# Conditioning vectors as row sums on VectorE, with an instruction order written out by hand

## The chip, the cores and the metric

The kernel runs on one core of a Trainium2 chip. The metric is the device time of one execution in microseconds (us), the median of several runs. A core has five engines that run side by side, each with its own queue in program order: TensorE (PE, matrix products; its weight loads are shown apart as PEld), VectorE (DVE), ScalarE (ACT), GpSimd (POOL) and SyncE (SP, which here sends the DMAs). All tensors are 32-bit floats. PE sums in PSUM, and everything else lives in SBUF with 128 partitions.

## The reference

One layer of a decoder trunk for one sequence of 512 tokens, width 1024. What matters here is the conditioning: a vector `c` of 1024 values gives six vectors of 1024.

```python
ada = (c @ w_ada[l] + b_ada[l])[:, None, :]          # w_ada: 1024 x 6144
sh1, sc1, gt1, sh2, sc2, gt2 = jnp.split(ada, 6, axis=-1)
h = rms_norm(x, norm1_w[l]) * (1.0 + sc1) + sh1
proj = h @ w_in[l]                                    # 1024 x 10016
...                                                   # two token mixers, gated
x = x + gt1 * ((g_att * y_att + g_rwkv * y_rwkv) @ w_o[l])
h = rms_norm(x, norm2_w[l]) * (1.0 + sc2) + sh2
x = x + gt2 * conv_ffn(h, w_up[l], conv_w[l], conv_b[l], w_down[l])
```

`sh1` and `sc1` are needed before the first product, `gt1` after the mixers, the rest still later. `w_ada` is 25 MB of a total of 127 MB that is read.

## The kernel before

**Products.** A 32-bit product is made of three: each operand is split into a high part (`hi`, rounded to a type that PE multiplies in one pass) and the remainder (`lo`), and `hi*hi`, `hi*lo` and `lo*hi` are summed in one PSUM bank. Splitting a weight tile costs a copy on ACT (`whi`) and a subtraction on DVE (`wlo`); the same is done to h (`hhi`, `hlo`). h is kept transposed, in eight chunks k of 128 features by 512 tokens.

**The start** (`start`, L608). x comes in four slices of 128 tokens, is normalised on ACT and DVE, and is turned on PE (`tr`). Meanwhile PE runs products on the identity whose result nobody reads (`warm`). `sh1` and `sc1` are made in four groups of two chunks: for a group eight DMAs of 256 KB bring w_ada rows (`araw`, L693, pieces of 1 KB), DVE multiplies each by its element of c and adds it to `acc` (L701, L703), and PE sums `acc` over the partitions with a column of ones (`ada<-few,acc`), which leaves a column per chunk; DVE adds the bias and makes `g1c` = (1 + sc1) * norm1_w (L727 to L729). ACT then makes a chunk of h from the turned x (L743) and `hhi` (L750), DVE makes `hlo` (L747), and the first products (`early`, L332 like all products) use each chunk as it comes, beside a part of the values (`v`).

**The other four vectors** (`ada_rest`, L512) are summed in the same way beside the attention part, from rows of 512 KB (L529, L531): for `sh2` and `sc2` again eight passes on PE, for the two gates four products with one output row each (`ada<-acc,few`), to which DVE adds the bias row before a DMA writes it to DRAM. The small vectors (biases, scales, convolution weights) come as rows from 17 DMAs and are turned into columns on PE (`vec`, L434 to L464).

**What sets the order.** Every step of the first two thirds is a task of a planner (`Plan`): engine, estimated duration, function, predecessors, priority, and buffers taken and given back. `Plan.run` plays the tasks through in time by the estimates and calls a task's function when its turn comes, which writes its instructions into the queues. `RANKS` moves the priority of named tasks, `HOLDS` holds back short PE steps (`few`) between long ones. On the chip each engine then runs its queue in that order, and semaphores keep the dependencies. The later parts (output projection, the gated MLP) are written in plain program order.

Of the kernel before, what the change touches and what calls it, by code (L numbers as in the profile page):

```python
# [39 lines left out]
class Task:  # L40
# [7 lines left out]
    ('ACT', '', '<lambda>', 200.0): -191.73,  # L48
    ('ACT', '', '<lambda>', 200.6): -134.73,
    ('ACT', '', 'l2_hi', 1.0): 88.76,  # L50
    ('ACT', '', 'r_hi', 200.1): 3.11,
    ('ACT', '', 'r_hi', 200.3): 21.71,
    ('ACT', 'exp', '<lambda>', 1.02): -19.52,
    ('ACT', 'exp', '<lambda>', 1.03): -33.04,
    ('ACT', 'gate hi', 'hi', 78.0): -74.13,
    ('ACT', 'k3 hi', 'hi', 49.0): 154.17,
    ('ACT', 'o', 'out', 1.03): 224.13,
    ('ACT', 'pr hi', 'hi', 88.0): -104.97,
    ('ACT', 'pts', 'turned', 1.0): 211.5,
    ('ACT', 'qk01', 'out', 1.0): 29.09,  # L60
    ('ACT', 'qk01 hi', 'hi', 12.0): 49.1,
    ('ACT', 'qk12 hi', 'hi', 17.0): -28.85,
    ('ACT', 'r4 hi', 'hi', 53.0): -52.65,
    ('ACT', 'v0 hi', 'hi', 42.0): 167.12,
    ('ACT', 'v12 hi', 'hi', 19.0): 218.37,
    ('ACT', 'v4 hi', 'hi', 54.0): 202.52,
    ('DMA', 'ada', 'load', 2.0): -35.02,
    ('DMA', 'ada', 'load', 3.0): -14.22,
    ('DMA', 'ada', 'load', 19.0): 1.45,
    ('DMA', 'ada', 'load', 25.0): -1.05,  # L70
    ('DMA', 'ada', 'load', 35.0): -1.19,
    ('DMA', 'gate', 'load', 64.0): 1.55,
    ('DMA', 'gate', 'load', 67.0): -2.21,
    ('DMA', 'gate', 'load', 68.0): 6.69,
    ('DMA', 'gate', 'load', 69.0): -6.31,
    ('DMA', 'gate', 'load', 73.0): 116.59,
    ('DMA', 'gate', 'load', 79.0): 160.33,
    ('DMA', 'lg', 'load', 38.0): -12.76,
    ('DMA', 'lg', 'load', 39.0): 1.1,
    ('DMA', 'pa', 'load', 81.0): 4.99,  # L80
    ('DMA', 'qk00', 'load', 4.0): -4.27,
    ('DMA', 'qk00', 'load', 5.0): -4.9,
    ('DMA', 'qk01', 'load', 11.0): -5.78,
    ('DMA', 'qk01', 'load', 25.0): -5.77,
    ('DMA', 'qk02', 'load', 29.0): 5.91,
    ('DMA', 'qk11', 'load', 27.0): 6.78,
    ('DMA', 'r7', 'load', 62.0): -1.38,
    ('DMA', 'rows', 'rows', 2.5): -19.57,
    ('DMA', 'rows', 'rows', 3.5): -7.21,
    ('DMA', 'v rows', 'v_load', 2.5): -6.43,  # L90
    ('DMA', 'v1', 'load', 45.0): -21.04,
    ('DMA', 'v2', 'load', 48.0): 13.86,
    ('DMA', 'v4', 'load', 54.0): -22.65,
    ('DMA', 'vec', 'load', 2.0): -50.64,
    ('DMA', 'x', 'load', 2.0): -53.8,
# [12 lines left out]
    ('DVE', 'ada', 'biased', 1.0): -46.21,
    ('DVE', 'ada', 'step', 1.5): 1.76,
    ('DVE', 'ada', 'step', 13.0): 32.5,  # L110
    ('DVE', 'ada', 'step', 15.0): 215.86,
    ('DVE', 'ada', 'step', 29.0): 61.6,
    ('DVE', 'pack', '<lambda>', 10.0): 154.57,
    ('DVE', 'qk01 lo', 'lo', 11.0): 43.99,
    ('DVE', 'qk01 lo', 'lo', 12.0): 19.2,
    ('DVE', 'qk02 lo', 'lo', 15.0): 160.78,
    ('DVE', 'qk10 lo', 'lo', 6.0): 20.02,
    ('DVE', 'r0 lo', 'lo', 41.0): -82.24,
    ('DVE', 'scan', '<lambda>', 200.1): -141.11,
    ('DVE', 'scan', '<lambda>', 200.4): -137.12,  # L120
    ('DVE', 'scan', '<lambda>', 200.7): -53.23,
    ('DVE', 'shift', '<lambda>', 1.0): 6.96,
    ('DVE', 'stat', '<lambda>', 1.02): -2.02,
    ('DVE', 'v lo', 'v_lo', 2.1): 43.03,
    ('DVE', 'v12 lo', 'lo', 19.0): -18.19,
    ('DVE', 'vec', '<lambda>', 1.0): 22.14,
    ('PE', '', '<lambda>', 0.0): -43.73,
    ('PE', 'early', '<lambda>', 10.6): 1.01,
    ('PE', 'gate', '<lambda>', 73.0): 6.63,
    ('PE', 'gate', '<lambda>', 75.0): -165.2,  # L130
    ('PE', 'gate', '<lambda>', 80.0): -14.65,
    ('PE', 'gate', '<lambda>', 81.0): 11.59,
    ('PE', 'gate', '<lambda>', 82.0): -91.61,
    ('PE', 'gate', '<lambda>', 83.0): 166.56,
    ('PE', 'gate', '<lambda>', 85.0): -83.89,
    ('PE', 'gate', '<lambda>', 87.0): 28.15,
    ('PE', 'k1', '<lambda>', 51.0): -49.98,
    ('PE', 'k3', '<lambda>', 57.0): 13.69,
    ('PE', 'pa', '<lambda>', 1.0): -0.19,
    ('PE', 'pa', '<lambda>', 90.0): -40.42,  # L140
    ('PE', 'pa', '<lambda>', 92.0): -19.64,
    ('PE', 'pa', '<lambda>', 95.0): 1.02,
    ('PE', 'pe', '<lambda>', 0.5): -74.3,
    ('PE', 'pe', 'first_pe', 0.5): -3.97,
    ('PE', 'pg', '<lambda>', 1.3): -85.89,
    ('PE', 'pg', '<lambda>', 1.4): -151.02,
    ('PE', 'pg', '<lambda>', 1.5): -8.13,
    ('PE', 'po', '<lambda>', 1.0): 2.71,
    ('PE', 'po', '<lambda>', 1.03): 3.37,
    ('PE', 'pt', '<lambda>', 1.4): 26.5,  # L150
    ('PE', 'pt', 'turn', 1.01): 0.03,
    ('PE', 'pt', 'turn', 1.02): 11.92,
    ('PE', 'pw', 'rates', 1.1): -1.11,
    ('PE', 'pw', 'rates', 1.2): 9.95,
# [2518 lines left out]
```

## Time and profile before

| | us |
|---|---|
| median of 3 runs | 1171.47 (1171.33 to 1172.0) |
| the profiled execution, its own time | 1172.75 |
| its span, first to last instruction | 1171.0 |
| w_ada in the chain that ended last | 2% of the span (DMA) |

A page of the profile gives each engine's busy time and number of instructions, then the chain of work that ended last, followed backwards. A group row reads: line, engine, operation, output and inputs, shapes, count | busy us, mean ns of one | idle time ahead of it and what ended it. A row of the timeline is: start, duration, engine, line, operation, names, count, and in brackets the idle time ahead. A row of stretches gives, for a window from A to B, the busy time of PE, PEld, DVE, ACT and POOL with their instructions, PE's granted clock, the share of the DMA engines and GB/s. A row of waits names who waited for whom: us in all, times, longest. Matmuls overlap, so their durations are longer than the distance between their starts.

### The profile page before, as it was taken

The numbers are of one execution on the slowest core, as the hardware profiler recorded it, in microseconds if no ns is written. First come the engines' busy times: TensorE is split into PE (matmuls) and PEld (weight loads), VectorE is DVE, ScalarE is ACT, GpSimd is POOL, SyncE is SP. The second block draws the span as 40 slices with busy tenths as digits, with TensorE's granted clock in tenths as the row PEclk, the third lists the DMA queues.
The fourth block names the chain that finished last, engine by engine and source line by source line (L and its number), as shares of the span: only waits on it lengthen the run. The fifth ranks groups of instructions, "written<-read, shape, count | busy, mean of one in ns | idle before, by whom it ended". The sixth has DMA issues, their size and how long they took to land.

```text
span 1171.0 us, 19239 instructions
## 1 busy us (share of the span) xinstructions
PE 1155.3 (99%) x7552; PEld 936.3 (80%) x7552; DVE 740.9 (63%) x1249; ACT 544.1 (46%) x1012; POOL 132.3 (11%) x271
## 2 busy tenths in 40 slices
PE   8999999999999999999999999999999999999997
PEld 8888888888788777777777777888888888888886
DVE  6788856324788978566997556744665666652236
ACT  5475433425476374464555653434444444432123
POOL 5010000000301013241002340023000000000001
PEclk9999999999999999999999999999999999999999
DMA  9765864111333332332243426621333333342231
GB/s 313 245 198 169 253 200 142 55 54 42 93 96 97 95 81 91 104 112 75 72 112 103 152 78 200 200 103 37 90 94 104 90 102 97 90 120 96 92 125 72
DMA packets 168330, 138.94 MB, mean 119 GB/s; under 512 B 8785, under 2 KB 150315, under 8 KB 168239
## 3 DMA queue, kind: packets, MB, share of 16 engines
q1 hardware_dynamic: 168095, 137.39, 38.7%
q8 instruction: 59, 0.97, 0.3%
q14 instruction: 32, 0.26, 0.1%
q10 hardware_dynamic: 144, 0.33, 0.1%
HBM read 127.39 MB, written 10.30 MB: 118 GB/s over the span
## 4 chain that ended last, share of the span: by engine, by line
PE 86%; DVE 7%; DMA 3%; issue 1%; ACT 1%; SPq 1%; POOL 0%; POOLq 0%; DVEq 0%; ACTq 0%
PE u L332 23%; PE o L332 13%; PE v L332 8%; PE qk L332 8%; PE pg L332 7%; PE pr L332 4%; PE k L332 4%; PE r L332 3%; PE pa L332 3%; DMA araw<-in_w_ada_dram 2%; PE pt L335 2%; PE xy L332 2%; PE sc L332 1%; PE xo L332 1%; PE po L332 1%
## 5 line engine op out<-in xcount | busy, mean ns | idle before, releaser
L378 DVE TENSOR_TENSOR wlo<-raw,whi 128x1024 fp32r<-128x1024 f32 x65 | 79.6, 1225 | 134.9 <-ACT whi L377 134.9
L332 PE MATMUL u<-h2hi,whi 128*128 128x512 f32 (+2 forms) x368 | 140.6, 382 | 0.0
L332 PE MATMUL u<-h2lo,whi 128*128 128x512 f32 (+2 forms) x368 | 140.6, 382 | 0.0
L332 PE MATMUL u<-h2hi,wlo 128*128 128x512 f32 (+2 forms) x368 | 140.5, 382 | 0.0
L1390 ACT CAST whi<-raw 128x1024 fp32r<-128x1024 f32 (+1 forms) x73 | 72.4, 993 | 103.4 <-PE qk L332 51.4
L377 ACT CAST whi<-raw 128x1024 fp32r<-128x1024 f32 x65 | 68.5, 1054 | 92.7 <-PE o L332 53.7
L1393 DVE TENSOR_TENSOR wlo<-raw,whi 128x1024 fp32r<-128x1024 f32 (+1 forms) x73 | 84.7, 1160 | 31.5 <-ACT whi L1390 30.6
L332 PEld LDWEIGHTS u<-h2lo,whi 128*128 128x128 f32 x368 | 69.1, 188 | 13.4 <-POOL h2lo L589 0.2
L332 PEld LDWEIGHTS u<-h2hi,wlo 128*128 128x128 f32 x368 | 69.1, 188 | 13.2
L332 PEld LDWEIGHTS u<-h2hi,whi 128*128 128x128 f32 x368 | 69.1, 188 | 12.9
L2488 DVE SCALAR_TENSOR_TENSOR u<-u,cols,u 128x511 f32<-128x511 f32 x88 | 65.7, 747 | 4.3 <-ACT u L2486 2.7
L332 PE MATMUL qk<-hhi,whi 128*128 128x512 f32 x160 | 63.3, 396 | 0.6 <-DVE qk L931 0.6
L332 PE MATMUL qk<-hhi,wlo 128*128 128x512 f32 x160 | 63.0, 394 | 0.0
L332 PE MATMUL qk<-hlo,whi 128*128 128x512 f32 x160 | 62.9, 393 | 0.0
L332 PE MATMUL o<-whi,fhi 128*128 128x512 f32 x144 | 56.1, 390 | 0.3 <-DVE u L2488 0.3
L332 PE MATMUL o<-wlo,fhi 128*128 128x512 f32 x144 | 56.0, 389 | 0.0
L332 PE MATMUL o<-whi,flo 128*128 128x512 f32 x144 | 56.0, 389 | 0.0
L332 PE MATMUL pg<-hlo,whi 128*128 128x512 f32 x128 | 52.0, 407 | 0.0
L332 PE MATMUL pg<-hhi,whi 128*128 128x512 f32 x128 | 51.6, 405 | 0.0
L332 PE MATMUL pg<-hhi,wlo 128*128 128x512 f32 x128 | 51.4, 403 | 0.0
L531 DVE SCALAR_TENSOR_TENSOR acc<-araw,cols,acc 128x1024 f32<-128x1024 f32 x28 | 35.9, 1282 | 17.6 <-DMA araw<-in_w_ada_dram 17.2
L2240 ACT CAST fhi<-u 128x512 fp32r<-128x512 f32 x22 | 13.7, 621 | 60.9 <-DVE u L2499 60.9
(462 smaller groups left out, 2776.3 us busy)
## 6 DMA issues: line engine op xcount, KB each, us to landing
raw<-in_w_in_dram SPq DMA_DIRECT2D x62, 512.0 KB
raw<-in_w_up_dram SPq DMA_DIRECT2D x44, 512.0 KB
araw<-in_w_ada_dram SPq DMA_DIRECT2D x32, 512.0 KB
raw<-in_w_down_dram SPq DMA_DIRECT2D x22, 512.0 KB
araw<-in_w_ada_dram SPq DMA_DIRECT2D x32, 256.0 KB
wvraw<-in_w_in_dram SPq DMA_DIRECT2D x20, 256.0 KB
raw<-in_w_rwkv_out_dram SPq DMA_DIRECT2D x8, 512.0 KB
raw<-in_w_o_dram SPq DMA_DIRECT2D x8, 512.0 KB
```

Source lines behind the costliest of these rows:

```text
L332: return self.nc.tensor.matmul(out, lhsT, rhs, start=start, stop=stop)
L335: self.nc.tensor.matmul(out, in_, self.ident[: in_.shape[0], : in_.shape[0]], is_transpose=True, start=start, stop=stop,)
L377: self.nc.scalar.copy(hl[0], raw)
L378: (lo_eng or self.nc.vector).tensor_tensor(hl[1], raw, hl[0], op=ALU.subtract)
L531: nc.vector.scalar_tensor_tensor(d["acc"], raw, ck, d["acc"], op0=ALU.mult, op1=ALU.add)
L1390: nc.scalar.copy(d["w"][0], d["raw"])
L1393: nc.vector.tensor_tensor(d["w"][1], d["raw"], d["w"][0], op=ALU.subtract)
L2240: self.nc.scalar.copy(hi, src)
L2488: nc.vector.scalar_tensor_tensor(u[:, d:], pu[:, : S - d], ch(c), u[:, d:], op0=ALU.mult, op1=ALU.add)
```

## The change

The two inputs are laid out before the launch (transposed and packed, no arithmetic): `w_ada` so that one output of the conditioning is one row of 1024 weights, 128 outputs to a slice of 512 KB; the small vectors as columns, in one array `vecs`, which two DMAs bring.

c is spread to all partitions (`cb`): a one-row load, two products with a row of ones, two copies on ACT. A slice of w_ada then gives 128 outputs in one DVE instruction, which multiplies by `cb` and adds along the row, starting from the bias (`ada_col`); a second, short instruction reads the accumulator out into the column. There is no `acc` and no `ada` product any more. `sh1` and `sc1` are made chunk by chunk, with two slices each. For k below 2 ACT writes `hhi` straight from PSUM, ahead of h itself; in the first group of weights the three products of a k are separate steps. `sh2` and `sc2` are put where `sh1` and `g1c` stood, and the gates go to DRAM as columns.

The planner still runs, but only to know which task runs on which engine: `AFTER` then moves single tasks behind others in an engine's list, and `MERGE`, a string with one letter a task, fixes in which order the engines' lists are written out. `RANKS` is another table. Smaller edits: one PSUM bank now holds `xy` and the state sum `w` and another `u`; `gt1b` is loaded earlier (in the gate stage, at m = 2); the first up products run in another order; the first eight down products too; 40 warming products and 12 more instead of 56.

```diff
 RANKS = {
-    ('ACT', '', '<lambda>', 200.0): -191.73,
...
 }
+AFTER = {
+    'ACT': (
+        "57:47 5:57 3:5 145:65 148:85 180:94 183:180 117:202 118:117 221:125 218:133 367:142 237:367 337:237 236:337 "
...
+MERGE = (
+    "dpddpppdapdpvagpdppadvgpappapdppppvpvpgdppvppappdpppavpvgpppdgappvpdppvpppdapppgapvpdapppdpvpappppppvadpppvpapp"
...
+    def issue(self, order):
+        for eng, moves in AFTER.items():
+            moves = [[int(x) for x in m.split(":")] for m in moves.split()]
+            moved = {u for u, _ in moves}
+            o = [t for t in order[eng] if t.uid not in moved]
+            for u, p in moves:
+                o.insert(o.index(self.tasks[p]) + 1 if p >= 0 else 0, self.tasks[u])
+            order[eng] = o
...
+        for c in MERGE:
+            t = next(next_[c])
+            assert not t.left, (t.uid, t.eng, t.name)
+            for u in t.users:
+                u.left -= 1
+            t.fn()
...
+    def ada_col(self, raw, col, m):
+        self.nc.vector.tensor_tensor_reduce(raw, raw, self.cb, 1.0, self.col["b_ada"][:, m : m + 1],
+                                            op0=ALU.mult, op1=ALU.add, accum_out=col)
...
     def ada_rest(self):
-                    nc.sync.dma_start(d["raw", k], self.w_ada[0][k * P : (k + 1) * P, part * D : (part + 1) * D])
+                    nc.sync.dma_start(d["raw", k], self.w_ada[part * KD + k])
...
-                        nc.vector.scalar_tensor_tensor(d["acc"], raw, ck, d["acc"], op0=ALU.mult, op1=ALU.add)
+                    self.ada_col(d["raw", k], d["col"][:, k : k + 1], part * KD + k)
...
-                        self.mm(d["ps"][:, j : j + 1], d["acc"][:, j * P : (j + 1) * P], self.ones[:, :1], j == 0, j == KD - 1)
...
-                        self.mm(d["ps", q][:1, :], self.ones[:, :1], d["acc"][:, q * 256 : q * 256 + 256], True, True)
...
+                prev = pl.add("DMA", 1.0, lambda d=d, name=name: nc.sync.dma_start(
+                    self.ada2[name][0].rearrange("(k p) -> p k", p=P), d["col"]), [prev], W_ + self.bodies, lag=2.0,
+                    marks=("att",), name="ada")
...
     def start(self):
+        def c_all(h):
+            d[h] = psp("cb")
+            self.mm(d[h], d["row"][:, D:], d["row"][:, h * 512 : h * 512 + 512], True, True)
...
-        STRAIGHT, PARTS = [(), (), (), ()], [(0, 2), (2, 4), (4, 6), (6, 8)]
...
-                self.mm(a["ps"][:, j : j + 1], a["acc"][:, j * P : (j + 1) * P], self.ones[:, :1], first and j == 0, j == m - 1)
...
+        for c in range(KD):
+            a, mine = {}, slice(c, c + 1)
+            for x, w in ((1, self.g1c), (0, self.sh1)):
+                def load(x=x, a=a, c=c):
+                    a[x] = sx.tile([P, D], F32, tag="araw", name=self.n("araw"), bufs=6)
+                    nc.sync.dma_start(a[x], self.w_ada[x * KD + c])
+                def step(x=x, a=a, w=w, c=c, mine=mine):
+                    self.ada_col(a[x], w[:, mine], x * KD + c)
...
+                    def hi_first(k=k, d=d, m=m, hf=hf):
+                        nc.scalar.activation(self.hhi[:, k, hf * m : (hf + 1) * m], d["ps"][:, :m], AF.Identity,
+                                             scale=self.g1c[:, k : k + 1], bias=self.sh1[:, k : k + 1])
...
+            if m == 2:
+                self.gt1b = mpool.tile([P, D], F32, name="gt1b", tag="gt1b")
+                nc.sync.dma_start(self.gt1b, self.ada2["gt1"].to_broadcast([P, D]))
...
+    a["w_ada"] = a["w_ada"][0].T.reshape(6 * KD, P, D)
```

How the order moves, at three places. First the queue of SP at the start, before (`xt` is a slice of x, `rows` a small vector, `raw` the first w_in rows):

```order
L648 DMA xt_147<-in_x_dram 128x1024
L648 DMA xt_151<-in_x_dram 128x1024
L648 DMA xt_155<-in_x_dram 128x1024
L648 DMA xt_162<-in_x_dram 128x1024
L452 DMA rows_174<-in_c_dram 8x128
L452 DMA rows_174<-in_b_ada_dram 48x128
L452 DMA rows_174<-in_norm_w_dram 8x128
L693 DMA araw_186<-in_w_ada_dram 128x2x256
```

Seven more like the last follow, and then `raw`. Now:

```order
L795 DMA c_row<-in_c_dram 1x1024
L824 DMA xt_150<-in_x_dram 128x1024
L824 DMA xt_152<-in_x_dram 128x1024
L824 DMA xt_158<-in_x_dram 128x1024
L867 DMA araw_164<-in_w_ada_dram 128x1024
L651 DMA cols<-in_vecs_dram 128x128
L824 DMA xt_178<-in_x_dram 128x1024
L867 DMA araw_191<-in_w_ada_dram 128x1024
L867 DMA araw_204<-in_w_ada_dram 128x1024
L926 DMA raw_216<-in_w_in_dram 128x2x256 x2
```

Three slices of w_ada instead of eight half slices stand ahead of the first weights, and one of them stands ahead of the last x slice.

Second, PE where the first products begin, before (`early` names one of four PSUM banks):

```order
L332 MATMUL early_366<-hhi,whi_324 128x512
L332 MATMUL early_366<-hhi,wlo_325 128x512
L332 MATMUL early_366<-hlo,whi_324 128x512
L332 MATMUL early_374<-hhi,whi_324 128x512
L332 MATMUL early_374<-hhi,wlo_325 128x512
L332 MATMUL early_374<-hlo,whi_324 128x512
```

and now:

```order
L540 MATMUL early_322<-hhi,whi_270 128x512
L540 MATMUL early_322<-hhi,wlo_271 128x512
L540 MATMUL early_325<-hhi,whi_270 128x512
L540 MATMUL warm_148<-ident 128x128
L540 MATMUL early_328<-hhi,whi_270 128x512
L540 MATMUL warm_148<-ident 128x128
L540 MATMUL early_328<-hhi,wlo_271 128x512
L540 MATMUL early_325<-hhi,wlo_271 128x512
L540 MATMUL warm_148<-ident 128x128
L540 MATMUL early_325<-hlo,whi_270 128x512
```

The products that need only `hhi` come first, across the banks, with warming products between; the one with `hlo` stood third and stands seventh among the products.

Third, PE in the attention part where the columns of `sh2` were summed, before (`sc` are attention scores):

```order
L332 MATMUL v_1552<-wvhi_1517,hlo 128x512
L332 MATMUL v_1552<-wvlo_1397,hhi 128x512
L332 MATMUL ada_1684<-few,acc_1297 128x1 x8
L332 MATMUL sc_1700<-pk_1313 128x256
L332 MATMUL sc_1701<-pk_1313 128x256
```

and the like place now:

```order
L540 MATMUL v_1381<-wvhi_1266,hhi 128x512
L540 MATMUL v_1381<-wvhi_1266,hlo 128x512
L540 MATMUL sc_1461<-pk_1326 128x256
L540 MATMUL sc_1462<-pk_1326 128x256
L540 MATMUL sc_1461<-pk_230a_1327,pk_1326 128x256
```

The eight passes are gone, and nothing has taken their place on PE.

More of the change, by code (lines that the diff above doesn't have):

```diff
@@ L60 @@
[L60 to L71, printed above, removed]
@@ L84 @@
[L84 to L95, printed above, removed]
@@ L120 @@
[L120 to L130, printed above, removed]
@@ new lines @@
+    ('ACT', 'qk12 hi', 'hi', 17.0): -25.51,
+    ('ACT', 'r3 hi', 'hi', 50.0): -55.49,
+    ('ACT', 'shift', '<lambda>', 1.0): -62.01,
+    ('ACT', 'v4 hi', 'hi', 54.0): -7.97,
+    ('DMA', '', 'y_load', 220.0): -153.95,
+    ('DMA', 'ada', 'load', 22.0): -36.35,
+    ('DMA', 'ada', 'load', 27.0): -1.5,
+    ('DMA', 'ada', 'load', 30.0): 8.87,
+    ('DMA', 'ada', 'load', 37.0): 11.49,
+    ('DMA', 'ada', 'load', 38.0): 25.87,
+    ('DMA', 'ada', 'load', 40.0): -1.79,
+    ('DMA', 'ada', 'load', 43.0): 24.99,
@@ new lines @@
+    ('DMA', 'ada', 'load', 44.0): 62.9,
+    ('DMA', 'ada', 'load', 46.0): 226.58,
+    ('DMA', 'gate', 'load', 66.0): -6.63,
+    ('DMA', 'gate', 'load', 67.0): -11.56,
+    ('DMA', 'gate', 'load', 71.0): -19.46,
+    ('DMA', 'gate', 'load', 73.0): 121.36,
+    ('DMA', 'gate', 'load', 74.0): 1.71,
+    ('DMA', 'gate', 'load', 79.0): 697.77,
+    ('DMA', 'k6', 'load', 58.0): -56.19,
+    ('DMA', 'k7', 'load', 61.0): 2.34,
+    ('DMA', 'lg', 'load', 38.0): -11.74,
+    ('DMA', 'lg', 'load', 39.0): 1.34,
@@ new lines @@
+    ('DMA', 'pa', 'load', 81.0): 7.47,
+    ('DMA', 'pa', 'load', 83.0): -4.97,
+    ('DMA', 'pa', 'load', 85.0): -66.74,
+    ('DMA', 'qk00', 'load', 5.0): -0.57,
+    ('DMA', 'qk01', 'load', 11.0): -4.77,
+    ('DMA', 'qk01', 'load', 12.0): 7.68,
+    ('DMA', 'qk11', 'load', 26.0): -13.41,
+    ('DMA', 'rows', 'rows', 4.5): -0.88,
+    ('DMA', 'v1', 'load', 45.0): -21.24,
+    ('DMA', 'v2', 'load', 48.0): 2.95,
+    ('DMA', 'x', 'load', 2.0): -20.35,
+    ('DVE', '', '<lambda>', 1.0): 0.17,
+    ('DVE', '', '<lambda>', 200.1): -193.84,
@@ L250, in run @@
                 push(0.0, 1, t)
-        few, since = False, 0.0
+        few, since, order = False, 0.0, {}
+        need = [t.left for t in self.tasks]
         done = 0
@@ L298, in run @@
                                                      for r in open_.values() for t in r][:20])
+        for t, n in zip(self.tasks, need):
+            t.left = n
+        self.issue(order)
+    def issue(self, order):
[6 more added lines that the diff above has]
+            order[eng] = o
+        names = dict(p="PE", v="DVE", a="ACT", g="POOL", d="DMA", n="NO")
+        next_ = {c: iter(order[e]) for c, e in names.items()}
+        for c in MERGE:
[4 more added lines that the diff above has]
+            t.fn()
+        assert len(MERGE) == len(self.tasks)
 C_, E_, W_, V_, I_, M_, S_, U_ = 0.0, 1.0, 2.0, 200.0, 200.15, 220.0, 1.0, 10.0
```

600 lines of the change are left out of this document (315 added, 285 removed), and 131 rows, old and new, of the table AFTER.

## The prediction

> **What bounds the kernel now.** I read the page first, then the waits of TensorE (PE), then busy time by stretches, then PE's timeline where a wait or an `ada` product stands.
>
> ```profile
> span 1171.0 us, 19239 instructions
> PE 1155.3 (99%) x7552; PEld 936.3 (80%) x7552; DVE 740.9 (63%) x1249; ACT 544.1 (46%) x1012; POOL 132.3 (11%) x271
> PE 86%; DVE 7%; DMA 3%; issue 1%; ACT 1%; SPq 1%; POOL 0%; POOLq 0%; DVEq 0%; ACTq 0%
> ...
> PE ada L332 <- DVE acc L703: 2.0, 3, 0.7
> ...
> 20.00:50.00 30.00, 28.56 (x168) 23.94 (x168) 26.67 (x44) 12.19 (x17) 3.53 (x10) 1.00 1.02 306
> 75.00:200.00 125.00, 124.11 (x742) 105.70 (x741) 91.46 (x156) 57.59 (x135) 4.14 (x12) 1.00 0.67 203
> 275.00:725.00 450.00, 447.96 (x3982) 339.67 (x3980) 331.32 (x644) 246.18 (x515) 90.73 (x171) 1.00 0.34 100
> 725.00:1046.00 321.00, 320.24 (x1461) 266.88 (x1461) 197.12 (x264) 141.57 (x209) 17.64 (x36) 1.00 0.34 102
> ```
>
> PE is busy 99% of the span and holds 86% of the chain that ended last. The longest wait PE has on another engine is for VectorE's (DVE's) `acc`, the sum of c times w_ada. In the stretch rows (PE, PEld, DVE, ACT, POOL, clock, DMA share, GB/s) PE is idle 1.44 us between 20 and 50, 0.89 between 75 and 200, 2.04 between 275 and 725 and 0.76 behind that; the granted clock is 1.00 in each. So time goes only where PE's useful work starts earlier, where a pass leaves PE, or where the few waits close. DVE is the second engine: 26.67 of 30 us while the first products are fed. (The profiled execution took 1172.75 us around its span of 1171.0; the median of the three timed runs is 1171.47. I subtract the sum from the span and carry the difference over to the median.)
>
> **The start.** Ahead of the first useful product PE does warming passes. It is released by data:
>
> ```profile
> 17.59 1.05 ACT L767 CAST whi<-raw 128x1024 fp32r<-128x1024 f32 x1 [5.14 <-DMA raw<-in_w_in_dram]
> 18.54 0.78 ACT L743 ACTIVATE ht<-tr,sh,g1c 128x512 f32<-128x512 f32 x1
> 19.35 0.62 ACT L750 CAST hhi<-ht 128x512 fp32r<-128x512 f32 x1
> 20.02 0.50 PE L332 MATMUL early<-hhi,whi 128*128 128x512 f32 x1
> ...
> 4.00:10.00 6.00, 5.46 (x44) 5.24 (x44) 1.81 (x5) 4.29 (x7) 1.90 (x3) 1.00 1.02 375
> 10.00:16.00 6.00, 6.00 (x55) 5.94 (x54) 5.29 (x9) 2.45 (x4) 5.28 (x10) 1.00 0.99 309
> ```
>
> ScalarE (ACT) sat 5.14 us waiting for the first w_in rows, with the DMA engines at a share of 1.0 all along. The queue of before sends 4 x 512 KB of x, 32 KB of small rows, 8 x 256 KB of w_ada and then the 512 KB of w_in: 4,640 KB. The new one sends 4 KB of c, four x slices, three w_ada slices of 512 KB, 64 KB of columns and the w_in rows: 4,164 KB, 0.49 MB less, which at 309 GB/s is 1.6 us. The three w_ada slices (1.57 MB) come in 4 KB rows like x, which moved at 375 GB/s, instead of 1 KB pieces, at 309: 5.1 less 4.2, 0.9 us. So the cast of `whi` starts at 17.6 - 2.5 = 15.1. After it, before needed scale (0.78) and cast (0.62) one behind the other; now `hhi` is written straight from PSUM: 0.62 less. First product at about 20.0 - 2.5 - 0.6 = 16.9: **-3.1 us**. Bounds: -0.6, if the bytes gain nothing, and -5.7, if all of ACT's 5.14 us of waiting closed. The spreading of c (two products on PE, two copies on ACT) I cost at nothing: it lies in the warming passes and in that wait of ACT. Without the wait, two copies as long as the 0.62 above would cost 1.2.
>
> It starts raggedly:
>
> ```profile
> 18.73 1.22 DVE L770 TENSOR_TENSOR wlo<-raw,whi 128x1024 fp32r<-128x1024 f32 x1
> 20.00 0.69 DVE L747 TENSOR_TENSOR hlo<-ht,hhi 128x512 fp32r<-128x512 f32 x1
> ```
>
> The list lets six products run before the first one with `hlo`, and DVE has the split of `whi` (1.2 us), a w_ada sum (about 1.3, priced below) and `hlo` (0.7) to do behind the cast that ends at 16.1: 19.3. Six products at 0.23 us are 1.4 of the 2.4 us between: **+1.0** (0 to +2.5, the whole of it).
>
> **The early sums leave PE.** Each group of two k ended in eight passes of `ada` for which PE waited:
>
> ```profile
> 25.65 0.39 PE L332 MATMUL early<-hlo,whi 128*128 128x512 f32 x1
> 26.74 1.05 PE L332 MATMUL ada<-few,acc 128*128 128x1 f32 x8 [0.70 <-DVE acc L703]
> 27.65 0.36 PE L332 MATMUL v<-wv,hhi 128*128 128x256 f32 x1
> ...
> 37.48 0.39 PE L332 MATMUL early<-hlo,whi 128*128 128x512 f32 x1
> 38.42 1.02 PE L332 MATMUL ada<-few,acc 128*128 128x1 f32 x8 [0.55 <-DVE acc L703]
> 39.30 0.37 PE L332 MATMUL v<-wv,hhi 128*128 128x256 f32 x1
> ...
> 47.95 0.95 PE L332 MATMUL ada<-few,acc 128*128 128x1 f32 x8
> 48.76 0.36 PE L332 MATMUL v<-wv,hhi 128*128 128x256 f32 x1
> ```
>
> From start to start, less the 0.23 of the product ahead (24 of them take 5.50 us in a row quoted with the rivals): 27.65 - 25.65 - 0.23 = 1.77, then 1.59, then 0.81 without a wait: **-4.2 us** (the one before 20 us is inside the start). Nothing hides these on PE. What is late next is DVE: a product of k now needs two row sums, k by k. DVE's work there hardly changes, so I keep the whole gain; if PE waits for each k instead, up to all 4.2 is lost (first rival).
>
> ```profile
> L531 DVE SCALAR_TENSOR_TENSOR acc<-araw,cols,acc 128x1024 f32<-128x1024 f32 x28 | 35.9, 1282 | 17.6 <-DMA araw<-in_w_ada_dram 17.2
> L703 DVE SCALAR_TENSOR_TENSOR acc<-araw,cols,acc 128x512 f32<-128x512 f32 x28 | 21.1, 752 | 1.1 <-DVE acc L703 0.2 <-DMA araw<-in_w_ada_dram 0.2
> L1036 DVE CUSTOM_DVE_ANT_0 sm<-sc,m 128x256 f32<-128x256 f32 x56 | 21.9, 420 | 14.1 <-PE sc L332 13.5 <-ACT pr L1042 0.2
> L1036 DVE DVE_READ_ACCUMULATOR2_ANT stat<- 128x1 f32 x64 | 5.3, 82 | 0.0
> L1036 DVE CUSTOM_DVE_ANT_0 sm<-sc,m 128x128 f32<-128x128 f32 x8 | 2.2, 288 | 0.9 <-ACT pr L1042 0.7 <-PE sc L332 0.2
> ```
>
> The new sum is the custom form of the third row, with its accumulator read. From 128 to 256 elements it grows by 132 ns, 1.03 ns an element, so 1024 elements take 0.288 + 896 x 0.00103 = 1.21 us, and 0.08 for the read: 1.29. The nearest row with two SBUF operands of this length is 1.28. I take 1.30 (1.21 to 2.5; the upper end is twice the rate's price, since the `sm` rows read one operand from PSUM and so do not show two SBUF operands with an accumulator). Early DVE work: 16 x 1.38 = 22.1 us and some small steps, against 21.1 in the L703 row, four first sums and small steps. Equal within the estimate.
>
> [...]
>
> **The later sums leave PE.**
>
> ```profile
> 108.88 1.02 PE L332 MATMUL ada<-acc,few 128*1 128x256 f32 x4
> 109.83 0.39 PE L332 MATMUL v<-wv,hhi 128*128 128x256 f32 x1
> ...
> 141.64 1.84 PE L332 MATMUL ada<-few,acc 128*128 128x1 f32 x16
> 143.34 0.48 PE L332 MATMUL sc<-pk 128*128 128x256 f32 x2
> ...
> 198.00 1.02 PE L332 MATMUL ada<-acc,few 128*1 128x256 f32 x4 [0.29 <-DVE row L564]
> 198.96 0.66 PE L335 MATMUL pt<-ident,pr 128*128 128x128 f32 x4
> ```
>
> Two groups like the one at 141.64 take 1.70 each (143.34 - 141.64), four like the others 0.95 (109.83 - 108.88), and 0.29 of waiting goes: 3.40 + 3.80 + 0.29 = **-7.5 us**. Bounds -7.5 and -3: PE is 124.11 of 125 busy there, so the passes are on the path, unless another wait opens in their place. DVE trades the 35.9 us of the L531 row, four first sums and the bias rows for 32 x 1.38 = 44, at most 8 more; it has 125 - 91.46 = 33.5 us idle in this stretch. The four turns of small vectors (`vec`), their DVE copies and the gates' writes in another shape I cost at nothing: PE's other work, 124 us of it, covers them, and the gates are read far later. Without cover the turns cost a pass each, 4 x 0.23 = 0.9. The edits behind 725 (the gate's earlier load, the first up products, the first down rows) can close only 0.76 us of idle time; nothing for them either.
>
> **The order.** The list moves hundreds of steps. Where PE idles 2.04 of 450 us, closing waits can win only that; but waits also hide in longer passes:
>
> ```profile
> L332 PE MATMUL u<-h2hi,whi 128*128 128x512 f32 (+2 forms) x368 | 140.6, 382 | 0.0
> L332 PE MATMUL qk<-hhi,whi 128*128 128x512 f32 x160 | 63.3, 396 | 0.6 <-DVE qk L931 0.6
> L332 PE MATMUL pg<-hlo,whi 128*128 128x512 f32 x128 | 52.0, 407 | 0.0
> ```
>
> The undisturbed `u` takes 382 ns, `qk` 14 more in 3 x 160 passes (6.7 us), `pg` 25 more in 3 x 128 (9.6). At best the order wins these 16 us, at worst it doubles them. The kinds and counts of products in the middle are the same and short steps stand between long ones in both, so I take **0** (-16 to +16, mostly within 8).
>
> **Sum.** -3.1 + 1.0 - 4.2 - 7.5 + 0 = -13.8: span 1157.2, profiled execution 1158.9, median 1171.5 - 13.8 = **1157.7 us**.
>
> **Rivals.**
>
> *The early part is paced by DVE and DMA.* For: DVE 26.67 of 30 and DMA at 306 GB/s, a share of 1.02, between 20 and 50. Against: w_ada in longer rows and DVE work that is no greater. Then PE starts early but waits at each k; the 4.2 and half of the net start of 2.1 go: 1157.7 + 5.2 = 1163. 15%.
>
> *The order closes half of the hidden waits*: 8 us off, 1150. For: the `pg` and `qk` rows above; against: each switch from long to short passes remains. 17%.
>
> *The sum runs at half rate* (slower side). It is 1.2 us dearer each. Early: 15 sums follow one another on a DVE without slack, +18.
>
> ```profile
> 50.09 0.16 DVE L729 SCALAR_TENSOR_TENSOR g1c<-g1c,cols 128x2 f32<-128x2 f32 x1
> ...
> 55.88 5.50 PE early L332 x24
> ```
>
> The last early products began 5.8 us after the last scale (the second row is of the chain of waits), so PE has that much other work: +12 of the 18. Later: 32 x 1.2 = 38 us against 33.5 idle: +5. 1157.7 + 17 = 1175. It becomes slower than before from about 2.35 us a sum on. Against it: 1.28 in the L531 row. 7%. [...]
>
> *The written order stalls in the middle* (slower side). PE's list cannot react; with only two `araw` buffers DVE waited 17.2 us for w_ada in before, and a late row sum now stands ahead of the split of weights that PE needs next. A stall of 0.5 us at each of the 32 sums gives 1157.7 + 16 = 1174; from 0.43 us each it is slower than before. Against: only 0.89 us of PE idle came of those waits so far. 6%.
>
> **How the numbers follow.** Forecast 55% (1157.7, own range 1152 to 1163), the rivals 15, 17, 7 and 6%. A difference under 0.2% (2.3 us) can't be told from none in this kernel. Faster takes the forecast, the first two rivals and little else: 0.86; slower both last rivals with most of their weight: 0.10; the same 0.04. The range: the low bound takes in half the order's gain and a better start, the high one the first rival and a rougher order: 1146 to 1167.
>
> **What would show it.** The first `early` product at 16 to 18 us; no `ada` on PE; the row sum at 1.2 to 1.4 us with 0.08 behind it; PE idle between 20 and 50 below 1.4 us; first `early` products of the last k before 50 us; PE idle between 75 and 200 no more than 1 us. Wrong it is if the sum takes 2 us or more, if PE shows waits for `hlo` or `g1c` of over 3 us before 55, or if `pg` passes grow longer than 407 ns.

## The result and the profile after

The changed kernel takes 1185.39 us (median of 4 runs, 1185.1 to 1187.41) where the kernel before takes 1171.48: a ratio of 1.0122, with a 95% interval from 1.0104 to 1.0139. It is 14 us slower, where the prediction had it 14 us faster (1157.7, with a range of 1146 to 1167). The page of the changed kernel opens thus (span, TensorE's busy time, the chain that ended last):

```profile
span 1183.4 us, 18950 instructions
PE 1161.4 (98%) x7452; PEld 930.6 (79%) x7452; DVE 736.1 (62%) x1263; ACT 539.2 (46%) x1014; POOL 130.7 (11%) x272
PE 47%; DVE 2%; issue 0%; ACT 0%; POOLq 0%; POOL 0%; DVEq 0%; ACTq 0%
```

TensorE has 100 instructions fewer and is busy 6 us longer. The chain could be followed back only as far as 582 us here (its shares add up to about half), so its 47% can't be set against the 86% of before. The waits of its engine (line, what it waited for, us in total, times, longest) and the stretches of the prediction:

```profile
PE qk L540 <- ACT qk L1113: 4.6, 1, 4.6
...
PE pg L540 <- DVE v L1587: 1.5, 1, 1.5
PE pg L540 <- DVE k L1587: 0.7, 1, 0.7
PE pg L540 <- DVE km L1673: 0.7, 1, 0.7
PE pb L540 <- DVE rl L1826: 0.5, 1, 0.5
```

```profile
20.00:50.00 30.00, 30.00 (x185) 26.44 (x184) 25.24 (x44) 13.10 (x19) 4.77 (x14) 1.00 0.88 305
75.00:200.00 125.00, 119.91 (x682) 101.60 (x680) 87.86 (x174) 56.35 (x135) 2.52 (x13) 0.97 0.70 204
275.00:725.00 450.00, 444.84 (x3950) 335.73 (x3951) 326.10 (x635) 239.97 (x511) 90.92 (x171) 1.00 0.34 99
725.00:1046.00 321.00, 320.02 (x1418) 260.03 (x1417) 194.65 (x261) 138.70 (x205) 17.07 (x36) 1.00 0.33 101
```

Between 20 and 50 us TensorE no longer idles. Between 75 and 200 it now idles 5.1 us (0.9 before), 4.6 of it in one wait, and its granted clock is 0.97. Between 275 and 725 it idles 5.2 us (2.0 before). The last row looks as before, but holds 1,418 matmuls where the row of before holds 1,461. Part of that is that the kernel comes there 5 us later and splits fewer of its first up products in two (12 matmuls); the rest is time lost inside the row.

The waits alone do not add up, so I worked out from both traces how late each kernel is when the same work is left to TensorE: all of its matmuls but the warming ones, the `ada`, `vec` and `cb` products, each weighted with the usual time from start to start of its size (227 ns for 512 columns). Both kernels have the same work, 1,068.6 us by these weights. Other weights for the short products move the rows in time; from 880 on the last column then holds to within 1.3 us.

| work left, us | before at | after at | after against before |
|---|---|---|---|
| 1000 | 91.9 | 88.1 | -3.8 |
| 960 | 134.7 | 134.8 | +0.1 |
| 880 | 224.1 | 219.8 | -4.3 |
| 760 | 348.9 | 347.1 | -1.8 |
| 560 | 577.6 | 578.9 | +1.3 |
| 400 | 752.6 | 757.7 | +5.1 |
| 160 | 1002.8 | 1012.4 | +9.6 |

The gain of the early part is there, and is lost in three places: at once near 130 us, bit by bit between 220 and 750, and evenly in the up-projection from 800 on. Each needs its own experiment.

### The profile page after: what moved, and what is told of

The parts are those of the page before. It is cut to its first block, busy times and chain, and to the rows that moved or that the text cites. A ratio compares the mean times of both kernels' runs of the same rounds, so it can differ in the third digit from the quotient of the medians.

```text
span 1183.4 us, 18950 instructions
## 1 busy us (share of the span) xinstructions
PE 1161.4 (98%) x7452; PEld 930.6 (79%) x7452; DVE 736.1 (62%) x1263; ACT 539.2 (46%) x1014; POOL 130.7 (11%) x272
## 5 line engine op out<-in xcount | busy, mean ns | idle before, releaser
L540 PE MATMUL u<-h2lo,whi 128*128 128x512 f32 (+2 forms) x364 | 143.2, 393 | 0.0
L540 PEld LDWEIGHTS u<-h2hi,whi 128*128 128x128 f32 x364 | 68.4, 188 | 16.4
L540 PEld LDWEIGHTS u<-h2lo,whi 128*128 128x128 f32 x364 | 68.4, 188 | 14.8
L694 DVE CUSTOM_DVE_ANT_0 araw<-araw,cb,cols 128x1024 f32<-128x1024 f32 x48 | 61.2, 1285 | 19.8 <-DMA araw<-in_w_ada_dram 19.7
L1226 ACT ACTIVATE pr<-sm,stat 128x256 f32<-128x256 f32 (+1 forms) x64 | 31.3, 490 | 27.3 <-PE pt L543 12.1
```

The costliest lines, as they stand in the source:

```text
L540: return self.nc.tensor.matmul(out, lhsT, rhs, start=start, stop=stop)
L694: self.nc.vector.tensor_tensor_reduce(raw, raw, self.cb, 1.0, self.col["b_ada"][:, m : m + 1], op0=ALU.mult, op1=ALU.add, accum_out=col)
L1226: nc.scalar.activation(d["pr"][h][:, :wd], d["sm", h][:, :wd], AF.Exp, bias=stt[gi][:, n, 0, hd(h) : hd(h) + 1], scale=-1.0, accum_out=stt ...
```

## Experiments

**The stall near 130 us: how the gates are written.** In the changed kernel, SyncE's queue and the transfers asked for between 110 and 130 us (the last number is the median us from issue to landing), then ScalarE, then TensorE:

```profile
112.56 0.58 SPq L723 DMA_DIRECT2D gt_d<-gcol  x1
113.23 5.99 SPq L1154 DMA_DIRECT2D wvraw<-in_w_in_dram  x4
...
wvraw<-in_w_in_dram SPq DMA_DIRECT2D x4, 256.0 KB, 11.9
gt_d<-gcol SPq DMA_DIRECT2D x1, 4.0 KB, 13.2
...
130.35 1.04 ACT L1165 CAST wvhi<-wvraw 128x1024 fp32r<-128x1024 f32 x1 [5.92 <-DMA wvraw<-in_w_in_dram]
...
132.90 0.80 PE L540 MATMUL qk<-hhi,whi 128*128 128x512 f32 x1 [4.58 <-ACT qk L1113]
...
113.00:126.00 13.00, 13.00 (x88) 11.21 (x86) 11.96 (x26) 8.11 (x22) 0.00 (x0) 1.00 0.78 100
126.00:135.00 9.00, 4.42 (x20) 3.64 (x18) 2.34 (x6) 3.80 (x7) 0.00 (x0) 0.78 0.81 258
```

A gate of 4 KB takes 13.2 us to land; as a column it goes to DRAM in 1,024 pieces of 4 bytes (1,084 of the 2,535 packets of 113 to 126 us are under 512 B). From 113 to 126 the DMA engines are busy at a share of 0.78 and move only 100 GB/s. The v weights right behind the gate in the queue are late; ScalarE stands 5.92 us at their cast, and behind that cast in its queue waits the copy that frees a PSUM bank for TensorE's next `qk`. TensorE stands 4.6 us, until 132.9, and its granted clock is 0.5 for 6.8 us, from 131.1 to 137.9. Two theories: the gate write does it, or the list asks for the loads too late anyway. The experiment turns the gate on VectorE first (the column is made 32 wide for that, filled up with zeros; the notes behind `#` are not in the code):

```diff
...
-                    self.ada2[name][0].rearrange("(k p) -> p k", p=P), d["col"])   # one DMA
...
+                    nc.vector.transpose(row, d["col"])                             # blocks of 32x32
+                    out = self.ada2[name][0].rearrange("(k b i) -> k b i", k=KD, i=32)
+                    for b in range(4):
+                        nc.sync.dma_start(out[:, b, :], row[32 * b : 32 * b + KD, :])
```

> The changed kernel with the two gate vectors turned by VectorE (blocks of 32x32) ahead of their write, so that each goes to DRAM in 32 pieces of 128 bytes and not in 1,024 pieces of 4 bytes; nothing is left out. Theory of the gate write: its small pieces fill the 16 DMA engines from 112.6 to 125.7 us, so the v weights behind it land at 127 to 130, ScalarE waits 5.9 us for them, TensorE stands 4.9 us at 127.8 and then runs 6.8 us at clock 0.5 (3.4 us lost); with few pieces the write lands in about 2 to 3 us, both losses go, and the time is 1185.4 - 8 = 1177 (1175 to 1180). Rival, the loads of that stretch are asked for too late by the list itself, whatever the gate write does: a TensorE wait of 3 us or more stays near 128 and the time is 1184 to 1186.

Measured: 1177.36 us (1176.4 to 1177.87), ratio 1.0041 (1.0027 to 1.0056). The same views of this run:

```profile
wvraw<-in_w_in_dram SPq DMA_DIRECT2D x4, 256.0 KB, 4.0
...
124.08 1.07 ACT L1172 CAST wvhi<-wvraw 128x1024 fp32r<-128x1024 f32 x1
...
113.00:126.00 13.00, 13.00 (x87) 11.26 (x86) 11.96 (x27) 9.02 (x23) 0.00 (x0) 1.00 0.82 269
126.00:135.00 9.00, 9.00 (x50) 7.78 (x52) 5.76 (x15) 6.69 (x19) 0.00 (x0) 1.00 0.19 63
```

The v weights land in 4.0 us, ScalarE does not wait, TensorE is busy for the whole 9 us at clock 1.00, and 8.0 us are back (9.5 by the two ratios). The gate write is the cause, with the wait (4.6) and the halved clock (TensorE is busy for 5.0 of its 6.8 us, so some 2.5 lost) as its two parts, about 7 of the 8.0. The second gate is written in the same way at 265.3 us, and there TensorE waits for nothing between 255 and 285, at clock 1.00: that write cost it nothing that shows. By work left, this kernel is 11.6 us ahead of before at 880 us left, where the changed kernel is 4.3 ahead.

**The up-projection: where the tiles lie.** TensorE's groups by form (busy, mean ns of one; the ends are modelled, so only differences count) and the number of matmuls in 180 us of the up-projection, first before, then after:

```profile
L332 PE MATMUL u<-h2lo,whi 128*128 128x512 f32 x336 | 130.7, 389 | 0.0
...
850.00:1030.00 180.00, 180.00 (x795) 149.02 (x794) 110.95 (x135) 77.80 (x99) 0.00 (x0) 1.00 0.33 97
```

```profile
L540 PE MATMUL u<-h2lo,whi 128*128 128x512 f32 x340 | 135.6, 399 | 0.0
...
850.00:1030.00 180.00, 180.00 (x773) 1.00 0.32 95
```

TensorE waits for nothing in either, at clock 1.00, and still 773 products fit where 795 did. From start to start they take 226.7 ns before and 233.3 after. The products are the same (but for four of each kind that the change no longer splits). What differs is where the tiles lie: three small tiles fewer (`sc2`, `sh2` and the old `g2c`) put the weight tiles 96 bytes lower in each partition, while `h2hi` and `h2lo`, allotted from the other end, stay. Theory: the addresses set the pace. Rival: the order or the clock does. The runs move the weight side (and all that is allotted behind it) by small amounts, by sharing or saving small tiles (the notes behind `#` are not in the code):

```diff
-        self.omu = scaled("mu", -1.0, 1.0)
-        self.omu2 = scaled("mu2", -1.0, 1.0)
+        both = cp.tile([P, 27], F32, name="omu")             # 32 bytes less
+        todo.append((both, self.cols[:, 1, :27], -1.0, 1.0))
+        self.omu, self.omu2 = both[:, :26], both[:, 26:27]
...
-        self.w0h = scaled("w0", 0.5, 0.0)
+        self.w0h = self.col["w0"]                            # 32 less, in place; so a0 (32), b_gate (64)
+        todo.append((self.w0h, self.w0h, 0.5, 0.0))
```

> The changed kernel with two small tiles of column vectors (mu and mu2) kept in one, so that the weight tiles, the normed input and all that is allotted behind them lie 32 bytes lower in SBUF; the tiles on the other side (the second normed input, the end weights, the y halves) stay. Nothing is left out. Theory of addresses: a 512-column product is slow (233 ns from start to start in the up-projection) where the moving tile and the next weight tile differ in address modulo 64, and fast (227 ns) where they agree; the shift makes them agree again, so the 1,008 up-projection passes fall from 233.3 to 226.7 ns (-6.7 us), the 84 end passes and the some 140 y passes by as much (-1.5), and the time is 1185.4 - 8 = 1177 (1175 to 1179). Rival, the order of the list or the clock makes the passes slow: 233 ns stays and the time is 1185 (1183.5 to 1187).

> As the run with the 32-byte shift, and one more small tile less (w0 is halved in place), so the same tiles lie 64 bytes lower than in the changed kernel. Theory of addresses modulo 64: weights and moving tiles still differ in the same 32 bytes, so the up-projection stays at 233 ns per pass and the time at 1185 (1183.5 to 1187). Rival, what counts is another distance, or any place but the one of the change is good: passes at 227 ns and 1177.

> The kernel before with mu and mu2 in one tile, so that its weight tiles lie 32 bytes lower; its order and everything else stay. Theory of addresses: its 1,008 up-projection passes go from 226.7 to 233.3 ns (+6.7 us), its end and y passes by +1.5 in all, time 1171.5 + 8 = 1179.5 (1177 to 1182). Rival, the slow passes of the changed kernel come from its order or clock: the kernel before stays at 1171.5 (1170 to 1173).

> The changed kernel with mu and mu2 in one tile and w0, a0 and b_gate halved in place, so the weights, the normed input and what lies behind them are 160 bytes lower; nothing is left out. With the 32-byte shift weights and moving tiles agreed modulo 64 but not modulo 256, and the up-projection only fell from 233.3 to 232.4 ns. Theory now: they must agree modulo 256, as all of them did in the kernel before (remainder 224 each); the 160 bytes restore that, so the up-projection passes are 226.7 ns, the end passes 226.7 and the y passes about 228, together -8.5 us: 1176.9 (1175 to 1179). Rival, addresses do not set it and the kernel before is fast for another reason (its order, the last tiles on the other side): passes stay at 232 to 234 ns and the time at 1183 to 1186.

Measured (each ratio is to runs of the kernel before on the same chip; ns from start to start over all `u<-h2` products; the remainder is that of the address of `h2hi` less the address of `whi`):

| kernel | remainder modulo 64 | modulo 256 | ns a product | time, us | ratio to before (95%) |
|---|---|---|---|---|---|
| before | 0 | 0 | 226.7 | 1171.5 | |
| changed | 32 | 96 | 233.3 | 1185.4 | 1.0122 (1.0104 to 1.0139) |
| changed, 32 lower | 0 | 128 | 232.4 | 1183.1 | 1.0089 (1.0073 to 1.0106) |
| changed, 64 lower | 32 | 160 | 234.3 | 1185.3 | 1.0111 (1.0096 to 1.0127) |
| before, 32 lower | 32 | 32 | 233.4 | 1180.5 | 1.0069 (1.0053 to 1.0084) |
| changed, 160 lower | 0 | 0 | 226.8 | 1178.1 | 1.0046 (1.0034 to 1.0057) |

The kernel before, moved by 32 bytes, becomes 8.4 us slower in its old order (1180.45 against 1172.09 of before on that chip): addresses it is. My first rule for them, agreement modulo 64, was wrong: with 32 bytes less the products stayed at 232.4. The second, agreement modulo 256, held in the run made for it, which restored 226.8 ns and 7.3 us (8.9 by the two ratios). That run's group and stretch:

```profile
L540 PE MATMUL u<-h2lo,whi 128*128 128x512 f32 x340 | 132.3, 389 | 0.0
...
850.00:1030.00 180.00, 180.00 (x795) 1.00 0.33 97
```

The end products (`o<-wehi` and its kin) went with them: 226.7 before, 233.5 after, 226.7 with 160 bytes less. Two controls agree. The down products (`o<-whi`), whose two tiles lie on the same side and move together, take 228.0 ns both before and after. And in the changed kernel the second pair of weight tiles (`whi`, `wlo`) lies in another place, where the remainder is 0: nine products with it start 227 ns apart, from 816.46 to 818.28 us, and the seven behind them, with the moved tiles, 233. What in the memory makes it so, these runs do not show. That 256 bytes is the unit rests on six kernels, two of which agree (their distances differ by 256, so 512 is not it).

**The start: warming passes ahead of the first turn.** The changed kernel's TensorE and ScalarE at the start:

```profile
3.16 3.78 PE L540 MATMUL cb<-c_row 1*128 1x512 f32 x4
6.86 9.65 PE L540 MATMUL warm<-ident 128*128 128x128 f32 x64
16.35 0.60 PE L543 MATMUL tr<-ident,xt 128*128 128x128 f32 x4
...
20.05 0.48 PE L540 MATMUL early<-hhi,whi 128*128 128x512 f32 x1
...
14.81 1.03 ACT L933 CAST whi<-raw 128x1024 fp32r<-128x1024 f32 x1
16.99 0.78 ACT L895 ACTIVATE hhi<-tr,sh,g1c 128x512 fp32r<-128x512 f32 x1 [1.15 <-PE tr L543]
```

The data came as early as predicted (`whi` at 14.8, predicted 15.1), but the first product ran at 20.05 as before (20.02): the first turn stands in the list behind the warming passes, which end at 16.4. The passes are also dear here. Before, TensorE starts with them:

```profile
1.45 7.46 PE L332 MATMUL warm<-ident 128*128 128x128 f32 x50 [1.45 <-POOL ident masks.py:199]
9.62 2.94 PE L332 MATMUL warm<-ident 128*128 128x128 f32 x24
```

From start to start a pass takes 213 ns until 4.8 us there and 112 from then on. In the changed kernel the products that spread c stand in between, 3.7 us of TensorE, and the passes take 213 ns until 11.5 us. That the c products keep them slow is an inference from these two starts; no run leaves the c products out.

The experiment leaves 28 of the 52 out:

```diff
-            t = pe(..., warm, [t], 50.0, name="warm")                                # 40 of them
+            t = pe(..., warm if i < 24 else lambda: None, [t], 50.0, name="warm")
-                            warmed = pe(0.12, warm, [t, warmed], 50.0, name="warm")  # 12 more
+                            warmed = pe(0.12, lambda: None, [t, warmed], 50.0, name="warm")
```

> The changed kernel without the last 16 of its 40 first warm passes and without the 12 behind the first turn; only warm passes are left out. Theory: the first turn waits for the warm passes ahead of it in the list (they end at 16.5 us, the last normed quarter of x is there at 14.9); without them the turn starts at 15.0, the first early product at 17 to 17.5 and not at 20.05, and the first qk product, or the end of the early products, 1.5 to 3 us earlier: 1183.2 (1181.5 to 1184.5). Rival: what follows is paced by VectorE and ScalarE (hlo, weights), so the first product comes earlier and the last k of the early part where it was: 1185.4 (1184.5 to 1187). A third outcome: TensorE then idles long enough for its clock to fall, and the time rises by 2 us or more.

Measured: 1185.96 us (1183.55 to 1188.66), no change. The first product runs at 16.93, and by work left the kernel is 2.8 us ahead of the changed one at 1000 us left and still 2.5 at 600 (530.6 against 533.1). So the time is the rival's, but not for its reason: the lead outlives the early part. Then it loses the lead in one place. Of this run, a wait of TensorE, three stretches around it (PE, granted clock, DMA share, GB/s), and the first product:

```profile
PE pe L540 <- issue: 1.8, 1, 1.8
...
645.00:653.00 8.00, 7.96 (x265) 1.00 0.29 89
653.00:657.50 4.50, 2.66 (x67) 1.00 0.19 55
657.50:664.50 7.00, 7.00 (x83) 0.52 0.73 227
...
16.93 0.50 PE L540 MATMUL early<-hhi,whi 128*128 128x512 f32 x1 [0.84 <-ACT hhi L895]
```

TensorE stands 1.84 us in a row of short products, for nothing that the profile shows, and has half its clock for 6.8 us after it. That loss belongs to this execution. The median does not move, so something takes the 3 us in the others as well. Part of it may be the clock: these four executions show a granted clock of 0.993 to 0.995, those of the changed kernel 0.995 to 0.996, and 0.001 of the span is 1.2 us (more with the last two runs).

**The list.** To see what the written list is worth, the planner's own order was issued with the same tables of ranks and holds:

```diff
-                order.setdefault(eng, []).append(t)
+                t.fn()
...
-        self.issue(order)
```

> The changed kernel with every task issued as its planner schedules it, that is without the written list and its moves; data, weights and addresses as changed, the planner's ranks and holds those of the change. Theory of the written list as worth little (0, as the prediction took it): 1185.4 with at most 8 us either way. Rival, the list closes waits that the planner leaves, and without it TensorE's waits of over 0.3 us grow by 8 us or more: 1194 or slower. A rival to the gate write as the cause of the half clock: without the list the stall near 128 is gone, and the time is below 1182.

Measured: 1237.69 us (1233.83 to 1244.6), ratio 1.0562. Two of its longest waits:

```profile
PE pt L540 <- ACT pr L1223: 10.9, 3, 8.0
PE qk L537 <- ACT qk L1110: 5.6, 3, 1.9
```

The list is worth 52 us against the planner with these ranks, so "worth little" is refuted, and so is the third outcome, a time below 1182. Not all of it is waits: the profiled execution has a granted clock of 0.980, against 0.995 in the changed kernel, and 0.015 of 1237 us is 18.6 us. But the ranks were made for the list, and this says nothing on how the new order stands against the old one. No run has the new tasks under the planner with the ranks of before.

**All three edits, and seven moves.** The gates turned, 160 bytes less and fewer warming passes together:

> The three edits in one kernel: the 160-byte shift, gates written in 32 pieces of 128 bytes, and the 28 warm passes left out. If the causes add: 1185.4 - 8.5 (addresses) - 8.0 (gate write, as measured alone) - 2 (first turn) = 1167 (1164 to 1170), faster than the kernel before (1171.5). If the first turn is hidden: 1169. If the addresses are not the cause: 1176.

Measured: 1170.4 us (1168.5 to 1173.61), ratio 0.9987 (0.9975 to 1.0): 15 us faster than the changed kernel, and just about the time of before. Gates and addresses add up (1185.4 - 8.0 - 7.3 = 1170.1; by the ratios, which are known to some 2 us, they would give 1167); the start adds nothing that shows. By work left this kernel is 14.2 us ahead of before at 880 us left and 2.5 at 400: between 210 and 750 us it loses 11.7, about 4 of them between 480 and 440 us left (665 to 716 us). The next two runs move seven tasks within the engines' lists, at TensorE's longest waits there (each number pair: a task, and the one that it is put ahead of):

```diff
+AHEAD = ((2309, 3626), (2793, 2794), (3052, 2785), (3087, 3107), (3088, 3054), (4042, 4001), (3403, 4017),)
+        for u, before in AHEAD:
+            seq.remove(self.tasks[u])
+            seq.insert(seq.index(self.tasks[before]), self.tasks[u])
```

> The kernel with all three edits and, on top, seven moves in the written list: VectorE's shift of v ahead of a weight part (TensorE stood 1.6 us before a gate product there), one piece of the inverse behind the shift of k (0.9), the low part of r and the shift of v earlier (0.5 and 0.8), and in the load queue one load of the last part behind the first g load of the pair, and the second g load ahead of a weight load (TensorE stood 1.5 and 0.7 us between 666 and 679). Theory: the list is not worth nothing, its new short waits between 330 and 700 us cost about 4.5 us, and the 3 us from the earlier first product vanish in the waits at 650 to 680 behind the g loads; with the moves 3 to 5 us of it come back: 1170.4 - 4 = 1166.4 (1164 to 1168.5), a ratio of 0.995 to before. Rival: each wait that is closed opens behind it another, the stretch is bound elsewhere (VectorE's chain): 1169.5 to 1171.5.

> The same kernel with all the warm passes back, so that the first early product is at 20 us and not at 17. Theory: with the g loads moved the 3 us of the start reach the end, so this kernel is 1.5 to 3 us slower than the one with fewer warm passes. Rival: they are absorbed behind 590 us in either list, and both have the same time within 0.5 us.

Measured: with fewer warming passes 1167.92 us (1166.95 to 1169.9), ratio 0.9969 (0.9957 to 0.9981), in the theory's range and faster than both kernels; with all of them 1169.34 (1168.08 to 1173.59), ratio 0.9983 (0.9975 to 0.9992). The two moves of g loads in the load queue bring what there is: 2.5 us ahead of before at 400 us left become 4.3. By work left the five moves around VectorE bring nothing (no run has them alone); where a wait closed, another opened. The waits of TensorE between 570 and 605 us and four stretches (PE, PEld, DVE, ACT, POOL, clock) of the faster of the two:

```profile
PE pg L546 <- DVE v L1604: 1.2, 1, 1.2
PE pg L546 <- DVE gt L1860: 1.1, 1, 1.1
...
570.00:577.00 7.00, 5.74 (x35) 4.36 (x34) 6.75 (x17) 1.62 (x2) 0.00 (x0) 1.00 0.16 38
577.00:581.00 4.00, 4.00 (x19) 3.28 (x18) 3.69 (x10) 1.50 (x3) 0.00 (x0) 1.00 0.22 67
594.00:601.00 7.00, 5.84 (x30) 4.72 (x29) 6.76 (x10) 1.11 (x3) 1.03 (x4) 1.00 0.31 77
601.00:605.00 4.00, 4.00 (x90) 2.96 (x89) 3.90 (x8) 3.56 (x6) 0.00 (x0) 1.00 0.00 0
```

VectorE is busy 6.75 of 7 us there: an earlier step of it only makes another one late, which is the rival's case for this stretch. The start's 2.5 us (17.2 against 19.7 for the first product) reach the end as 1.4 by the medians, between the theory's 1.5 to 3 and the rival's 0.5; the two intervals of the ratio overlap.

## Why the prediction was wrong

The passes that leave TensorE brought about what was forecast. What failed are three terms that stood at nothing: the gates' writes (8.0 us), the pace of products that the change leaves alone (7.3 to 8.4) and the new order of the middle part (about 9, of which the cause is open in the main).

**The start (-3.1).** Its chain of data was right: with 28 warming passes fewer the first product ran at 16.93, predicted 16.9. The step that failed is "The spreading of c (two products on PE, two copies on ACT) I cost at nothing: it lies in the warming passes". The c products took 3.7 us of TensorE, from 3.16 to 6.86 us, and the warming passes behind them 213 ns each until 11.5 us. The prediction counted the passes as cover; in a fixed list they are work that the first turn waits for, so "It is released by data" failed with it: the first turn came at 16.35, when the passes ended; with fewer of them it was through by 16.1, its last pieces released by x at 15.3. I did not follow the list from the data to the turn. By work left, start, ragged start and early sums should have brought -3.1 + 1.0 - 4.2 = -6.3 us; they brought -3.8, and -6.6 with fewer passes. So the early terms were right in size together, in the kernel with fewer passes. At the end of the kernel the start was worth 0 (changed list) to 1.4 us (with the moves).

**The later sums (-7.5).** Right: with the gates turned, the lead grows from 3.9 us (1000 left) to 11.6 (880 left), 7.7. What took it away is a term that stood as nothing: "the gates' writes in another shape I cost at nothing: PE's other work, 124 us of it, covers them, and the gates are read far later". I looked at who reads the gates, not at what stands behind the write in the same queue. It cost 8.0 us.

**The order (0).** Between 880 and 400 us left the kernel with turned gates falls from 11.6 us ahead to 2.1: that is a loss of about 9 us, inside the bounds of 16 that were set for the order and a little outside "mostly within 8". No run separates the order from the other edits in this stretch, such as the PSUM bank that `xy`, `w` and another `u` now share. In the profiles TensorE's waits between 270 and 720 us are 4.8 us after and 1.3 before, so some 3.5 us of the 9 are waits that can be named. Seven moves brought about 2 us of it back. What the rest is stays open. It is spread: from start to start, waits included, `v` and `pg` lose 2.3 to 2.4 us each there, `qk`, `k` and `xy` with `u` about 1 each.

**What the sum had no term for.** "The undisturbed `u` takes 382 ns" was taken as a property of the product. In these runs it was one of the product and its addresses: the change took three small tiles away, and 1,008 products became 6.6 ns slower (226.7 to 233.3 from start to start), 6.7 us, with the end and y products 7.3 to 8.4 us by the runs. "Nothing for them either", of the edits behind 725, failed with it. The agreement modulo 256 could not be read from the profile of before; that the tiles moved could be read from the change.

**The row sum (1.30 + 0.08).** Right, though the rows that it was worked out from read only one operand from SBUF:

```profile
L694 DVE CUSTOM_DVE_ANT_0 araw<-araw,cb,cols 128x1024 f32<-128x1024 f32 x48 | 61.2, 1285 | 19.8 <-DMA araw<-in_w_ada_dram 19.7
```

No run shows the doubled price that bounded the estimate (2.5 us, the third rival's case): with two operands in SBUF the sum took 1,285 ns with accumulator, near the 1,210 by the slope of the shorter rows and far from twice that. Two operands without accumulator took 1,282 before.

**The rivals.** VectorE and DMA do not pace the early part: TensorE idles 0 of 30 us (some of them warming passes). A stall did come in the middle, but one, of 4.6 us, behind a DMA write, and none at the 32 sums. The order did not shorten the `pg` passes (405 to 408 ns, 403 to 407 before, so one of the three rows passed the 407 that was named as a sign of being wrong). Of the signs, the missing `ada`, the sum's price and the idle time of 20 to 50 came true. The first product (20.05, not 16 to 18), the first products of the last k (52.3, not before 50) and the idle time of 75 to 200 (5.1, not 1) did not.

**The sum by what the runs show:** -3.8 (start and early part) - 7.7 (later sums) + 8.0 (gate write) + about 9 (the middle part) + 7.3 to 8.4 (addresses) = +12.8 to +13.9, measured 13.9.

## What to carry to other kernels

A small transfer's price was not its bytes here but its pieces (13.2 us for 4 KB in 1,024), and it was paid by what stood behind it in the queue (v weights that took 11.9 us to land, 4.0 with the gate in 32 pieces): turning a vector that was kept as a column on chip before it went to DRAM, ahead of loads that were needed soon, brought 8.0 us. When a change adds or removes tiles, compare the addresses of the operands of the longest matmul loops before and after, and look at the time from start to start there: here it showed the difference (226.7 and 233.3 ns), and busy time (180.00 of 180 us in both kernels) and waits (none in either) did not. Follow a fixed list from the data to the first instruction that needs it: here the warming passes that were counted as cover held the first turn until 16.35 us; with 28 fewer it began at 14.39.

## What was not expected of the hardware

- The 512-column float32r products of the up-projection took 226.7 to 226.8 ns from start to start in the two kernels where the addresses of the moving and the weight tile agreed modulo 256, and 232.4 to 234.3 in the four where they did not, at granted clock 1.00 from 850 to 1030 us in all six. The down products, whose two tiles moved together, kept their pace (228.0).
- A write of 4 KB in 4-byte pieces took 13.2 us, and the core's DMA traffic was at 100 GB/s from 113 to 126 us, where 269 GB/s moved in the same 13 us with the gate in 32 pieces.
- TensorE's granted clock was at half behind waits much shorter than the one of 4.6 us, and not in each execution: for 6.8 us behind the wait of 1.84 us in the run with fewer warming passes, and at 1.00 behind the two waits of 1.2 and 1.1 us in the faster run with the seven moves, shown above. The run with all warming passes and the seven moves has the same two waits, and in its profiled execution the clock was halved for 3.4 us behind each (0.57 over 4 us):

```profile
577.00:581.00 4.00, 4.00 (x14) 3.06 (x12) 3.79 (x11) 0.00 (x0) 0.00 (x0) 0.57 0.48 131
...
601.00:605.00 4.00, 4.00 (x13) 3.20 (x13) 3.86 (x6) 1.51 (x4) 1.02 (x4) 0.57 0.14 43
```

The halved stretches were 3.4 us long in this run and 6.8 us in the changed kernel and the run with fewer warming passes. What decides whether the clock falls behind such a wait, and for how long, was not shown. Where it fell behind a wait of 1.1 to 1.84 us, it cost 1.7 or 3.4 us on top of the wait (an estimate: half of 3.4 or 6.8). The longer runs show the lower clock: in the kernel with all three edits the run of 1168.5 us has a granted clock of 0.998, the one of 1173.61 us 0.994.
